# Sliding-window copy: staging in sets of 16 blocks, one per engine, instead of whole batches

## The chip, the cores and the metric

The kernel runs on one core of one Trainium2 chip. The metric is the device time of one execution in microseconds (us); the number that counts is the median of several runs. A core has compute engines (TensorE, VectorE, ScalarE, GpSimd) and a SyncE, and sixteen DMA engines that move all data. SyncE (SP), ScalarE (ACT) and GpSimd (POOL) each start DMAs into a ring of their own; all rings are served by the same sixteen DMA engines. In the profile q1 is SP's ring and q10 is ACT's.

## The reference

x has 32 batches of 4096 rows of 256 float32. A window is 64 rows, the next one starts 32 rows later, so there are 127 windows a batch. The output holds every window in full:

```python
n_windows = (length - window_size) // stride + 1          # 127
for i in range(n_windows):
    start = i * stride
    result[:, i] = x[:, start:start + window_size].copy()
```

Nothing is computed; data is copied. If a batch is cut into 128 blocks of 32 rows (32 KB each), window i consists of blocks i and i+1. Every block but the first and last is written twice: as the second half of one window and as the first half of the next. x is 134 MB, the output 266 MB.

## The kernel before, in words

There are two ways to move a batch, and both run side by side.

*Copied batches* go from HBM to HBM. A window's 64 KB are contiguous in x and in the output, so the copy of a batch is 127 rows of 64 KB whose source rows overlap. It reads 8.32 MB and writes 8.32 MB. `copy` starts three DMAs on SP's ring: 80, 32 and 15 rows, cut into packets of 16, 32 and 16 KB (`COPY_PARTS`, parts of a 64 KB row). A DMA spreads its rows over the DMA engines.

*Staged batches* go through on-chip memory (SBUF). One DMA loads the batch's 128 blocks, one block to a partition (4.19 MB), and two DMAs store the same tile: once as the windows' first halves, once as their second halves, shifted by one block (`half` 0 and -1). A staged batch thus reads 4.19 MB and writes 8.39 MB of HBM, and the DMA engines carry 12.58 MB. All of it is on ACT's ring, in packets of 16 KB. There are five tiles (`BUFS`), each with the semaphores `loaded[i]` and `stored[i]`.

The two stores of a staged batch also write one block beyond it at each end: half -1 of block 0 falls into the last window of the batch before, and half 0 of block 127 into the first window of the batch after it, both with wrong data. So the batches beside a staged one have to be copied after it is stored, or mended afterwards:

- `STAGED` holds the odd batches 1 to 23 (12 of them); the even batches beside them are `near`.
- The four in `EARLY` (18, 20, 22, 24) are copied first of all. Before ACT stores a batch that borders on one, it waits for all early copies. In the end the spoilt half windows (32 KB each) of these are written again, "mended", by seven small DMAs on SP's ring (`g.half`).
- The other near batches are "tied": SP waits for the stores of their staged neighbours (`after_store`) before it copies them. `_order` puts them into SP's list between the free batches, each at a place by when its neighbours should be stored.

ACT's program is a loop over the staged batches: load n+1, wait for load n, store n twice. A load into a tile that was used before waits for its earlier batch's stores. SP's program is the list of copies with the waits of the tied ones, then the mends, then waits for everything and the clearing of the semaphores. Each DMA, when done, adds 16 to its semaphore in all (at most one small completion packet of 4 bytes on each engine).

Of the kernel before, what the change touches and what calls it, by code (L numbers as in the profile page):

```python
# [1 line left out]

# [4 lines left out]


STAGED = tuple(range(1, 24, 2))
BUFS = 5  # L10

EARLY = (18, 20, 22, 24)

BLOCK_PARTS = 2

COPY_PARTS = ((80, 4), (32, 2), (15, 4))


class _Geometry:


    def __init__(self, x, out, W, S):
        self.B, self.L, self.D = x.shape
        self.x, self.out = x, out
        self.n_win = (self.L - W) // S + 1
        self.n_blk = self.L // S
        self.blk = S * self.D
        self.win = W * self.D
        assert W == 2 * S and self.n_blk == self.n_win + 1 == 128

    def src(self, b, block, dims):

        at = (b * self.n_blk + block) * self.blk
        return bass.AP(self.x.tensor, self.x.offset + at, dims)

    def dst(self, b, half, dims):

        at = b * self.n_win * self.win + half * self.blk
        return bass.AP(self.out.tensor, self.out.offset + at, dims)

    def rows(self, b, w0, n):

        s, d = [[self.blk, n], [1, self.win]], [[self.win, n], [1, self.win]]
        return self.dst(b, 2 * w0, d), self.src(b, w0, s)

    def half(self, b, half, block):

        dims = [[self.blk // 16, 16], [1, self.blk // 16]]
        return self.dst(b, half, dims), self.src(b, block, dims)


class _Kernel:
    def __init__(self, nc, g, tiles):
        self.nc, self.g, self.tiles = nc, g, tiles
        self.loaded = [nc.alloc_semaphore(f"loaded{i}") for i in range(len(tiles))]
        self.stored = [nc.alloc_semaphore(f"stored{i}") for i in range(len(tiles))]
        self.copied = nc.alloc_semaphore("copied")
        self.early = nc.alloc_semaphore("early")
        self.count = {}

    def start(self, engine, out, in_, sem, parts=1):
        engine.dma_start(out=out, in_=in_, max_dma_last_dim=65536 // parts).then_inc(sem, 16)
        self.count[id(sem)] = self.count.get(id(sem), 0) + 16

    def all_of(self, engine, sem):
        engine.wait_ge(sem, self.count[id(sem)])

    def slot(self, n):
        return divmod(n, len(self.tiles))

    def after_store(self, engine, n):
        turn, i = self.slot(n)
        engine.wait_ge(self.stored[i], 32 * (turn + 1))

    def load(self, n):

        g, (_, i) = self.g, self.slot(n)
        if n >= len(self.tiles):
            self.after_store(self.nc.scalar, n - len(self.tiles))
        src = g.src(STAGED[n], 0, [[g.blk, g.n_blk], [1, g.blk]])  # L80
        self.start(self.nc.scalar, self.tiles[i][:, :], src, self.loaded[i], 2 * BLOCK_PARTS)

    def store(self, n):

        g, (turn, i) = self.g, self.slot(n)
        self.nc.scalar.wait_ge(self.loaded[i], 16 * (turn + 1))
        for half in (0, -1):
            dst = g.dst(STAGED[n], half, [[g.win, g.n_blk], [1, g.blk]])  # L90
            self.start(self.nc.scalar, dst, self.tiles[i][:, :], self.stored[i], 2 * BLOCK_PARTS)

    def copy(self, b, sem):

        w = 0
        for rows, parts in COPY_PARTS:
            self.start(self.nc.sync, *self.g.rows(b, w, rows), sem, parts)
            w += rows
        assert w == self.g.n_win


def _order(B):


    near = {b for s in STAGED for b in (s - 1, s + 1)}
    order = list(EARLY) + [b for b in range(B) if b not in near and b not in STAGED]
    tied = sorted(near - set(EARLY))
    n = len(order) + len(tied)
    for b in tied:
        behind = max(STAGED.index(s) for s in (b - 1, b + 1) if s in STAGED)  # L110
        order.insert(-(-(2 * behind + 5) * n // (2 * len(STAGED))), b)
    return order


@with_exitstack
def kernel(
    ctx: ExitStack,
    tc: tile.TileContext,
    x: bass.AP,
    window_size: bass.AP,  # L120
    stride: bass.AP,
    out: bass.AP,
):
    nc = tc.nc
    W, S = int(window_size), int(stride)
    g = _Geometry(x, out, W, S)
    assert 0 not in STAGED and g.B - 1 not in STAGED
    pool = ctx.enter_context(tc.tile_pool(name="blocks", bufs=1))
    tiles = [pool.tile([g.n_blk, g.blk], x.dtype, name=f"xb{i}") for i in range(BUFS)]

    with tc.tile_critical():
        k = _Kernel(nc, g, tiles)
        for b in _order(g.B):
            if b not in EARLY:
                for s in (b - 1, b + 1):
                    if s in STAGED:
                        k.after_store(nc.sync, STAGED.index(s))
            k.copy(b, k.early if b in EARLY else k.copied)
        k.load(0)
        waited = False  # L140
        last = len(STAGED) - 1
        for n, s in enumerate(STAGED):
            if n < last:
                k.load(n + 1)
            if not waited and (s - 1 in EARLY or s + 1 in EARLY):
                k.all_of(nc.scalar, k.early)
                waited = True
            k.store(n)


        k.all_of(nc.sync, k.early)
        for n, s in enumerate(STAGED):
            if s - 1 in EARLY or s + 1 in EARLY:
                k.after_store(nc.sync, n)
            if s - 1 in EARLY:
                k.start(nc.sync, *g.half(s - 1, 2 * g.n_win - 1, g.n_blk - 1), k.copied)
            if s + 1 in EARLY:
                k.start(nc.sync, *g.half(s + 1, 0, 0), k.copied)
        for n in range(len(STAGED)):
            k.after_store(nc.sync, n)  # L160
        k.all_of(nc.sync, k.copied)
        for sem in [*k.loaded, *k.stored, k.copied, k.early]:
            nc.sync.sem_clear(sem)


# [1 line left out]
_INS = ['x', 'window_size', 'stride']  # L167
_OUTS = [((32, 127, 64, 256), 'float32')]

_NUMBERS = {'window_size': 64, 'stride': 32}  # L170


# [26 lines left out]
```

## Time and profile before

| What | Value |
|---|---|
| median of 3 runs | 766.97 us (766.28 to 768.57) |
| profiled execution | 768.4 us |
| its span, first to last instruction | 766.6 us |
| bytes moved by the DMA engines | 317.70 MB |
| HBM read / written | 217.02 / 267.35 MB |
| mean rate of the DMA engines | 414 GB/s |
| SP's issues | 20 each of 5120, 2048 and 960 KB, and 7 of 32 KB |
| ACT's issues | 12 loads and 24 stores of 4096 KB |

How to read it: a row of digits gives, for 40 equal slices of the span, the busy share of the sixteen DMA engines in tenths. For each DMA queue the page lists packets (the small completions among them), megabytes and the time that the packets took as a share of sixteen engines' span. The view by windows gives for each stretch the busy time of the compute engines, the granted clock (of no weight here), the DMA engines' busy share, where 1.00 is all sixteen, and GB/s. A wait of the queue's view reads: who waited, on which line, for which DMA; us in total, times, longest.

### The profile page before, as it was taken

The numbers are of one execution on the slowest core, as the hardware profiler recorded it, in microseconds if no ns is written. First come the engines' busy times: TensorE is split into PE (matmuls) and PEld (weight loads), VectorE is DVE, ScalarE is ACT, GpSimd is POOL, SyncE is SP. The second block draws the span as 40 slices with busy tenths as digits, with TensorE's granted clock in tenths as the row PEclk, the third lists the DMA queues.
The fourth block names the chain that finished last, engine by engine and source line by source line (L and its number), as shares of the span: only waits on it lengthen the run. The fifth ranks groups of instructions, "written<-read, shape, count | busy, mean of one in ns | idle before, by whom it ended". The sixth has DMA issues, their size and how long they took to land. (4 is left out here: it accounts for less than half of the span.)

```text
span 766.6 us, 180 instructions
## 1 busy us (share of the span) xinstructions
POOL 0.2 (0%) x4
## 2 busy tenths in 40 slices
POOL 0000000000000000000000000000000000000000
DMA  8999999999999999999999999999999999999996
GB/s 371 425 410 421 405 428 431 408 411 427 423 415 421 431 415 425 432 408 416 427 420 417 431 420 420 423 428 410 414 427 419 422 428 418 417 428 421 420 406 237
DMA packets 19837, 317.70 MB, mean 414 GB/s; under 512 B 1628, under 2 KB 1628, under 8 KB 1740
## 3 DMA queue, kind: packets, MB, share of 16 engines
q1 hardware_dynamic: 10044, 166.70, 51.9%
q10 hardware_dynamic: 9792, 151.00, 47.3%
q14 instruction: 1, 0.01, 0.0%
HBM read 217.02 MB, written 267.35 MB: 632 GB/s over the span
## 5 line engine op out<-in xcount | busy, mean ns | idle before, releaser
L180 POOL MEMSET const-bfloat16-1.0<- 128x1 bf16 x1 | 0.1, 102 | 0.0
L180 POOL MEMSET const-uint8-127<- 128x1 uint8 x1 | 0.1, 102 | 0.0
L180 POOL MEMSET const-float32-0.0<- 128x1 f32 x1 | 0.1, 99 | 0.2 <-issue 0.2
L180 POOL MEMSET const-float32-1.0<- 128x1 f32 x1 | 0.1, 99 | 0.0
## 6 DMA issues: line engine op xcount, KB each, us to landing
out_dram<-in_x_dram SPq DMA_DIRECT2D x20, 5120.0 KB, 114.8
out_dram<-xb ACTq DMA_DIRECT2D x24, 4096.0 KB, 84.6
xb<-in_x_dram ACTq DMA_DIRECT2D x12, 4096.0 KB, 123.2
out_dram<-in_x_dram SPq DMA_DIRECT2D x20, 2048.0 KB, 116.7
out_dram<-in_x_dram SPq DMA_DIRECT2D x20, 960.0 KB, 97.7
out_dram<-in_x_dram SPq DMA_DIRECT2D x7, 32.0 KB, 48.3
```

Source lines behind the costliest of these rows:

```text
L180: nc = _bacc.Bacc("TRN2", target_bir_lowering=False, num_devices=1)
```

## The change

Staging is cut finer. The unit is a set of 16 blocks, every eighth block of a batch (`STEP = 8`, partitions j, j+8, ...), 512 KB, so that one block of 32 KB goes to each DMA engine, as one packet. A batch is eight loads of a set and sixteen stores of one. `_staged` writes out ACT's order: after each load of a set two stores of sets follow, and the loads run ahead of the stores by `AHEAD = 12` sets. There are 13 staged batches (1 to 25), so 19 copied ones, and `EARLY` moves to 20, 22, 24, 26.

A copied batch is now three DMAs on SP's ring of 48, 32 and 32 rows in packets of 16 KB (`GROUPS`, `COPY_PARTS = 4`), and a fourth of its last 15 rows on GpSimd's ring in packets of 32 KB (`copy_others`, `OTHER_PARTS = 2`). GpSimd's DMAs wait for the neighbours as SP's do, and also for a staged batch's stores that paces them (`SLACK = 2`).

The two sets of the last staged batch that spoil its neighbours are stored first of that batch, with a semaphore of their own (`fringe`), and the mends beside that batch wait for that alone. In the end GpSimd, not SP, waits for all semaphores, resets its DMA queue and clears the semaphores in one go.

```diff
-STAGED = tuple(range(1, 24, 2))
+STAGED = tuple(range(1, 26, 2))
 BUFS = 5
-EARLY = (18, 20, 22, 24)
-BLOCK_PARTS = 2
-COPY_PARTS = ((80, 4), (32, 2), (15, 4))
+EARLY = (20, 22, 24, 26)
+STEP = 8
+AHEAD = 12
+GROUPS = (48, 32, 32)
+COPY_PARTS = 4
+OTHER_PARTS = 2
+SLACK = 2
...
-    def start(self, engine, out, in_, sem, parts=1):
+    def start(self, engine, out, in_, sem, parts=2):
         engine.dma_start(out=out, in_=in_, max_dma_last_dim=65536 // parts).then_inc(sem, 16)
...
-        engine.wait_ge(self.stored[i], 32 * (turn + 1))
-
-    def load(self, n):
+        engine.wait_ge(self.stored[i], 2 * 16 * STEP * (turn + 1))
+
+    def load(self, n, j):
         g, (_, i) = self.g, self.slot(n)
-        if n >= len(self.tiles):
+        if j == 0 and n >= len(self.tiles):
             self.after_store(self.nc.scalar, n - len(self.tiles))
-        src = g.src(STAGED[n], 0, [[g.blk, g.n_blk], [1, g.blk]])
-        self.start(self.nc.scalar, self.tiles[i][:, :], src, self.loaded[i], 2 * BLOCK_PARTS)
-
-    def store(self, n):
-        g, (turn, i) = self.g, self.slot(n)
-        self.nc.scalar.wait_ge(self.loaded[i], 16 * (turn + 1))
-        for half in (0, -1):
-            dst = g.dst(STAGED[n], half, [[g.win, g.n_blk], [1, g.blk]])
-            self.start(self.nc.scalar, dst, self.tiles[i][:, :], self.stored[i], 2 * BLOCK_PARTS)
+        src = g.src(STAGED[n], j, [[STEP * g.blk, g.n_blk // STEP], [1, g.blk]])
+        self.start(self.nc.scalar, self.tiles[i][j::STEP, :], src, self.loaded[i])
+
+    def wait_load(self, n):
+        turn, i = self.slot(n)
+        self.nc.scalar.wait_ge(self.loaded[i], 16 * STEP * (turn + 1))
+
+    def store(self, n, j, half, sem=None):
+        g, (_, i) = self.g, self.slot(n)
+        dst = g.dst(STAGED[n], half + 2 * j, [[STEP * g.win, g.n_blk // STEP], [1, g.blk]])
+        self.start(self.nc.scalar, dst, self.tiles[i][j::STEP, :], sem or self.stored[i])
 
     def copy(self, b, sem):
         w = 0
-        for rows, parts in COPY_PARTS:
-            self.start(self.nc.sync, *self.g.rows(b, w, rows), sem, parts)
-            w += rows
+        for n in GROUPS:
+            self.start(self.nc.sync, *self.g.rows(b, w, n), sem, COPY_PARTS)
+            w += n
+
+    def copy_others(self, b, sem):
+        w = sum(GROUPS)
+        self.start(self.nc.gpsimd, *self.g.rows(b, w, self.g.n_win - w), sem, OTHER_PARTS)
...
+def _copies(k):
+    nc, order = k.nc, _order(k.g.B)
+    for c, b in enumerate(order):
+        early = b in EARLY
+        if not early:
+            for n in _beside(b):
+                k.after_store(nc.sync, n)
+        k.copy(b, k.early if early else k.copied)
+        paced = c * len(STAGED) // len(order) - SLACK
+        for n in sorted({n for n in [paced] if n >= 0} | set([] if early else _beside(b))):
+            k.after_store(nc.gpsimd, n)
+        k.copy_others(b, k.early_others if early else k.others)
+
+
+def _staged(k):
+    nc, last = k.nc, len(STAGED) - 1
+    loads = [(n, j) for n in range(len(STAGED)) for j in range(STEP)]
+    stores = [(n, j, half) for n in range(last) for j in range(STEP) for half in (0, -1)]
+    fringe = [(last, STEP - 1, 0), (last, 0, -1)]
+    stores += fringe + [(last, j, half) for j in range(STEP) for half in (0, -1) if (last, j, half) not in fringe]
+    given = 0
+    waited = False
+    for s, (n, j, half) in enumerate(stores):
+        while given < len(loads) and 2 * given <= s + 2 * AHEAD:
+            k.load(*loads[given])
+            given += 1
+        if s % (2 * STEP) == 0:
+            if not waited and any(b in EARLY for b in (STAGED[n] - 1, STAGED[n] + 1)):
+                k.all_of(nc.scalar, k.early)
+                k.all_of(nc.scalar, k.early_others)
+                waited = True
+            k.wait_load(n)
+        k.store(n, j, half, k.fringe if (n, j, half) in fringe else None)
...
+def _end(k):
+    for sem in k.sems:
+        k.all_of(k.nc.gpsimd, sem)
+    k.nc.gpsimd.dma_reset()
+    used = sorted(sem.num for sem in k.sems)
+    assert used == list(range(used[0], used[-1] + 1))
+    k.nc.gpsimd.sem_clear(range(used[0], used[-1] + 1))
```

The function that is left out, `_mends`, holds the mends as they were, with the wait for `fringe` in place of that for the last batch's stores.

## The prediction, made before the changed kernel was run

> **What bounds the kernel now.** I read the page first. No compute engine does any work; the sixteen DMA engines are the kernel.
>
> ```profile
> span 766.6 us, 180 instructions
> DMA  8999999999999999999999999999999999999996
> DMA packets 19837, 317.70 MB, mean 414 GB/s; under 512 B 1628, under 2 KB 1628, under 8 KB 1740
> q1 hardware_dynamic: 10044, 166.70, 51.9%
> q10 hardware_dynamic: 9792, 151.00, 47.3%
> HBM read 217.02 MB, written 267.35 MB: 632 GB/s over the span
> ```
>
> They are busy 99% of the span, so no ring starves: time is bytes divided by rate, plus the two ends. q1 is SP's ring (copies), q10 ACT's (staging). Per byte both are equally dear, yet a staged batch moves 12.58 MB through the engines (one load, two stores) and a copied one 8.32 MB, although the copy costs HBM more (16.65 against 12.58 MB). The question is therefore at what rate the bytes go. The windows tell, once it is known which DMA ACT's ring is in. I counted q10's packets in order (256 data and 16 completions each); the order of issue is load n+1, store n, store n again.
>
> ```profile
> core 0: us, POOL busy (x), PEclk, DMA share, GB/s
> 0.00:6.00 6.00, 0.20 (x4) 1.00 0.68 246
> 6.00:20.00 14.00, 0.00 (x0) 1.00 1.01 432
> 83.00:104.00 21.00, 0.00 (x0) 1.00 1.00 410
> 105.00:125.00 20.00, 0.00 (x0) 1.00 1.01 431
> 146.00:167.00 21.00, 0.00 (x0) 1.00 1.01 404
> 168.00:189.00 21.00, 0.00 (x0) 1.00 1.02 431
> 209.00:231.00 22.00, 0.00 (x0) 1.00 1.00 408
> 232.00:251.00 19.00, 0.00 (x0) 1.00 1.00 429
> 722.00:748.00 26.00, 0.00 (x0) 1.00 0.94 401
> 753.00:764.00 11.00, 0.00 (x0) 1.00 0.59 216
> ```
>
> Windows from 83, 146 and 209 are loads; 105, 168 and 232 are first stores. The share is 1.00 in both, so in load windows the packets themselves take longer. A 16 KB packet takes 611 ns in the clean windows (start to start 607 ns, a 32 KB one 1209 ns); in load phases single packets take 1000 to 1400 ns, the copies' too. The packet records show that the two rings take turns packet by packet, and that a 4-byte completion takes a turn of its own of 6 ns (its record is 9 ns long).
>
> The span adds up. 317.70 MB at 432 GB/s: 735.4 us. Start, 6 us at 246: 2.6 lost. End, 11 us at 216: 5.5, and 2.6 after 764. From about 720 to 753 only fifteen engines work (401 GB/s): 2.4. Together 748.5; the other 18.1 are slow packets in the body: eleven loads, 235 us at about 409, lose 12.5; the first stores, 246 us at 430, lose 1.1; the second stores have the remaining 4.5, mostly in the last 2 us before the ring changes to a load.
>
> Why fifteen engines: q1's 10044 packets are 20 x 444 for copies, 112 for mends, and 1052 completions = 40 x 16 + 7 x 16 + 20 x 15. So each 15-row DMA uses 15 engines, the same ones each time by the idle end.
>
> **The change, part by part.**
>
> *Bytes.* 19 x 8.323 + 13 x 12.583 + 0.23 = 321.95 MB; at 432 GB/s 745.3 us, 9.9 more than now. This is certain and works against the change.
>
> *Completions.* Per engine 312 on ACT, 57 + 7 on SP, 19 on GpSimd: 395 against 103, at 6 ns: 1.8 us more.
>
> *Turns.* 32 KB and a completion on ACT's ring take two turns, in which SP's gets two 16 KB packets: equal bytes, as today. SP has 31 turns a batch, 589 in all; ACT 624. SP's ring runs out first, with some 17 sets (21 us) of stores left to ACT's alone. Today it is the other way round: the end is copies alone, at 216 GB/s while engines finish one by one between 759 and 764. Stores alone ask HBM for half of what copies do; I take 3 us for 5.5 (bounds 2 and 6). The last mends now wait for two sets put first, not for the whole last batch; today's land at 764.8, but other copies run until 763.2, so this gives 1.6 us at most and is in the 3.
>
> *The 15 rows.* If GpSimd's DMAs go round the engines, 2.4 us falls to about 0.5; if they use the same fifteen, 19 x 2 packets x 1.21 us / 16 = 2.9. No POOL DMA is in this trace. With nothing to choose by I take the middle, 1.7, and keep both for the range. [...]
>
> *Issue and waits.* ACT issues 312 DMAs for 36. A store's issue took 378 to 625 ns, so 120 to 195 us of the span, one each 0.6 us at worst where the ring needs one each 2.43 us: hidden. ACT's wait for a set's load has behind it the next sixteen stores, but fifteen sets (36 us of ring) were queued after that load: covered. SP's waits for a stored batch: batch k is stored after 24k+36 sets, at about 58k + 89 us; the copy tied to it comes to SP's ring at 38 us a batch, at least 45 us later in every case (k=9: 612 against 657). SP's existing waits total tens of us in the queue's view and leave the share at 1.00, for the same reason. GpSimd's waits hold only its own 15-row copies, the last of which is free at about 670 us.
>
> ```profile
> SPq L62 <- DMA out_dram<-xb: 61.2, 2, 40.2
> SPq L73 <- DMA out_dram<-xb: 19.2, 3, 9.4
> ```
>
> [...]
>
> *The close.* The queue is reset on GpSimd, which no row shows. Twelve semaphore clears now take 0.7 us. 2.6 becomes 3.5 (bounds 2.2 and 6).
>
> Sum without the body's loss: 745.3 + 1.8 + 2.6 + 3.0 + 1.7 + 3.5 = 757.9 us, against 748.5 today.
>
> *The body's loss, x.* Today loads and stores come in stretches of 20 and 40 us. Half the traffic is copies, so HBM reads and writes are 432 and 216 GB/s in a load stretch, 216 and 432 in a store stretch; mixed as one load to two stores they are 288 and 360. So x is bounded by today's rows: first stores' rate, 0.5% of 720 us, 3.4; all stores, (1.1 + 4.5) / 497, 1.1%, 8; no gain, 18 (what a loss linear in the reads gives too); load stretches' rate, 5.3%, 38. I take 5: 288 is nearer to the clean row, copies suffer too in load stretches (so it is the read load, not the load's own address), and the 4.5 of second stores comes mostly from the change to a load, whose reads then run on for 20 us; one set's reads last 1.2 us.
>
> Span 757.9 + 5 = 762.9. The profiled execution took 768.4, 1.8 over its span and 1.4 over the median of 766.97. So 764.7 beside the profiled 768.4, and 763.3 as median.
>
> **The rivals.**
>
> *No gain from mixing.* x stays at 14 to 20: median 772 to 778. For it: a linear loss; 32-row copies at 32 KB were slow even in store stretches. Against it: first stores lose almost nothing.
>
> *Changes of direction (slower).* Before a load the engines read from HBM for the load while they still write the store. At 82.4 to 83.8 us every packet took 650 to 800 ns: about 0.3 us lost at one change. Now each engine changes 104 times. If all sixteen do it together, 104 x 0.3 = 31 us: 757.9 + 3.4 + 31 is a span of 792.3, a median of 792.7. Spread over the 7.3 us of a load and two stores it costs nothing. It decides the sign where it costs over 766.6 - 757.9 - 3.4 = 5.3 us, 0.05 a change, a sixth of the price. Against lockstep: engines end up to 5 us apart today.
>
> *It doesn't do what it says.* The 15 rows stay on fifteen engines (1.2 us over what I took), and GpSimd's turns raise the copies' part: its two 32 KB packets a batch and engine are 19 x 2 x 1.21 = 46 us of copies, and beside them HBM is asked for more than the mix; at the load stretches' 5.3% that is up to 2.4 us more. Median 764.5 to 767.
>
> **How the numbers follow.** About 0.3% (2.3 us) can be told from no change: under 764.7 is faster, over 769.3 slower. The forecast has 0.55 (0.48 faster, 0.07 same), no gain 0.22, changes of direction 0.13, the last 0.10 (0.02 faster, 0.07 same, 0.01 slower). So faster 0.50, same 0.14, slower 0.36. The forecast's own range is 758 to 767. The whole range must take in no gain: 757 (x near 0 and an even spread of the 15 rows) to 777.
>
> **What would show it.** Right: the windows lie flat at 425 to 431 GB/s with no 20 us dips; q10 has 9984 data-and-completion packets and 163.6 MB; the last 20 us have q10 alone; POOL's ring has 18.2 MB. Wrong: flat windows at or under 420 (changes of direction), a DMA share under 0.98 in the windows of the body (a ring ran dry), or a close over 6 us.

## The result and the profile after

The changed kernel takes 795.76 us (median of 5 runs, 793.61 to 798.17) against 766.97 for the kernel before: a ratio of 1.0377, 95% interval 1.035 to 1.0403. It is slower by 29 us. The forecast was 763.3, with a range up to 777. The profiled execution took 798.17 us, with a span of 796.1.

The page of the changed kernel: the busy digits of the DMA engines, their rate in 40 slices of 19.9 us, the totals and the queues (packets, MB, share of sixteen engines' span). q0 is GpSimd's ring.

```profile
span 796.1 us, 475 instructions
DMA  9999999999999999999999999999999999999994
GB/s 304 344 389 430 424 416 422 429 426 422 434 424 414 424 429 423 430 426 417 431 430 424 431 427 412 428 429 425 431 429 411 427 427 422 424 426 426 351 238 102
DMA packets 20548, 322.00 MB, mean 404 GB/s; under 512 B 6359, under 2 KB 6359, under 8 KB 6471
q10 hardware_dynamic: 9984, 163.60, 51.6%
q1 hardware_dynamic: 9648, 139.69, 41.6%
q0 software_dynamic: 912, 18.68, 5.8%
```

Packets and bytes on every ring are those of the prediction (GpSimd's 18.68 MB where it said 18.2, which had taken 960 KB for 0.96 MB). The engines did not run dry either: the digits are 9 up to the last slice. But the middle is flat at 411 to 434 and the loss stands in the first three slices and the last three. The windows (length, GpSimd's busy time, clock, DMA share, GB/s) show it closer:

```profile
0.00:20.00 20.00, 2.04 (x7) 1.00 0.92 306
20.00:40.00 20.00, 0.00 (x0) 1.00 0.98 339
60.00:80.00 20.00, 0.00 (x0) 1.00 1.01 431
60.00:700.00 640.00, 8.64 (x15) 1.00 1.01 425
742.00:760.00 18.00, 0.00 (x0) 1.00 1.03 298
762.00:776.00 14.00, 0.00 (x0) 1.00 1.01 246
```

The share is 1.01 at 246 GB/s: the engines are occupied all the time, with packets that take up to twice as long. The kernel before ran at 421 from 60 to 700 us. So the body's rate did rise, by 1%; the two ends lose far more.

From 762 to 776 us the rings show who is there:

```profile
q10 hardware_dynamic: 202, 3.31, 98.1%
q1 hardware_dynamic: 128, 0.13, 2.7%
```

ACT's ring is all but alone, with stores of sets. A 32 KB store takes 2168 ns there on average in the packet records (median 2458), where the median is 1213 in the body. In the first 45 us, where ACT's ring holds loads of sets only, a load takes 1570 to 2490 ns (mean of a set), although SP's and GpSimd's packets go between.

The span in one sum, from the packet records. "Slow packets" is the time of packets over 611 ns (16 KB), 1213 (32 KB) and 84 (2 KB), divided by sixteen engines; "rest" is engines that end unevenly, and before the change the engine without 15-row copies.

| us | before | changed |
|---|---|---|
| first packet starts | 2.0 | 2.3 |
| bytes at 432 GB/s | 735.4 | 745.2 |
| completions (6 ns a turn) | 0.6 | 2.4 |
| slow packets, 0 to 80 us | 2.5 | 9.8 |
| slow packets, 80 to 720 us | 15.6 | 10.0 |
| slow packets, from 720 us | 1.2 | 17.5 |
| rest | 6.5 | 6.6 |
| last packet ends | 763.8 | 793.9 |
| to the span's end | 2.8 | 2.2 |

Of 30 us, 9.9 are bytes, 1.8 completions, 7.3 slow packets at the start and 16.3 at the end; the body gives 5.6 back.

### The profile page after: what moved, and what is told of

It reads as the page before. It is cut to its first block, busy times and chain, and to the rows that moved or that the text cites. A ratio compares the mean times of both kernels' runs of the same rounds, so it can differ in the third digit from the quotient of the medians.

```text
span 796.1 us, 475 instructions
## 1 busy us (share of the span) xinstructions
POOL 11.3 (1%) x23
## 3 DMA queue, kind: packets, MB, share of 16 engines
q0 software_dynamic: 912, 18.68, 5.8%
## 4 chain that ended last, share of the span: by engine, by line
another core or an unknown queue 44%; ACTq 30%; DMA 14%; issue 1%; SPq 0%
ACTq L75 30%; DMA xb<-in_x_dram 14%; ACTq L98 0%; ACTq L251 0%; SPq L215 0%
## 5 line engine op out<-in xcount | busy, mean ns | idle before, releaser
L75 POOL DMA_DIRECT2D out_dram<-in_x_dram x19 | 11.1, 583 | 696.9 <-DMA out_dram<-xb 695.8
```

## The experiments

Three causes could make packets slow at both ends. *Completions*: a ring that is alone must wait after each packet for its completion. *Distance*: sixteen engines work on blocks 256 or 512 KB apart and meet in HBM. *Packet size*: 32 KB packets are slow alone.

**Patterns alone, and beside copies.** Two kernels, each run once, held nothing but stretches of 8.39 MB on ACT's ring, the second with 112 rows of a batch's copy beside each. A stretch is written as

```python
for j in range(step):                                  # step 0: eight sets of 16 adjoining blocks
    dma(tile[j::step, :], x_block(b, j::step), parts)  # loads; step 1 is a whole batch in one DMA
```

> Twelve stretches on ACT's ring alone, one after the other, each 8.39 MB in 32 KB blocks; it moves only these blocks and no copies. Loads: sets of every eighth block in 32 KB packets; whole batches in 32 KB packets; whole batches in 16 KB packets; sets of 16 adjoining blocks; sets of every eighth block in 16 KB packets. Stores: the same first four, then sets of every fourth block (two packets before a completion), sets of every eighth in 16 KB packets, sets of every second block (four packets before a completion). At 432 GB/s a stretch lasts 19.4 us. Completion theory: a ring that is alone waits after each packet that is followed by a completion, about 1.3 us as in the changed kernel's last stretch (2.54 us for a 1.21 us packet). Then sets take 16 x 2.5 = 40 us whatever the distance of the blocks and the packet size, every fourth block about 30, every second about 25, whole batches 20 to 22. Distance theory: sixteen engines on blocks 256 or 512 KB apart at the same time meet in HBM. Then whole batches, which have the same distance between engines, are as slow as the sets (40 us), and adjoining blocks take 20. Packet theory: 32 KB packets are slow alone: everything in 32 KB takes 40, everything in 16 KB 20.

The windows of the kernel with ACT's ring alone (GB/s last; the edges of a stretch are cut off), in the order of the text above:

```profile
3.00:43.00 40.00, 0.00 (x0) 1.00 0.95 198
45.00:65.00 20.00, 0.00 (x0) 1.00 0.93 400
67.00:87.00 20.00, 0.00 (x0) 1.00 0.96 410
89.00:160.00 71.00, 0.00 (x0) 1.00 0.97 113
163.00:203.00 40.00, 0.00 (x0) 1.00 1.01 210
206.00:246.00 40.00, 0.00 (x0) 1.00 0.94 197
248.00:267.00 19.00, 0.00 (x0) 1.00 0.97 414
269.00:288.00 19.00, 0.00 (x0) 1.00 1.01 428
290.00:351.00 61.00, 0.00 (x0) 1.00 0.88 131
353.00:372.00 19.00, 0.00 (x0) 1.00 1.03 442
375.00:415.00 40.00, 0.00 (x0) 1.00 0.97 203
417.00:436.00 19.00, 0.00 (x0) 1.00 0.97 414
```

All three causes fall. Over its whole stretch a set of every eighth block runs at 207 GB/s, loads and stores alike, in 32 and in 16 KB packets: not the packet size. Adjoining blocks, which were to be the cure, are slowest, at 117 and 136: not the distance. Whole batches, at 403 to 423, say less of it than was meant: the records name no partition and no address, so which blocks the engines hold at one moment is not known. Sets of adjoining blocks have as many completions as sets of every eighth and run at 117 and 136 for 207, and 32 blocks in one DMA (every fourth block), with one completion for two packets, run at 426 instead of the 280 that a wait of 1.3 us a completion would give: not completions. What orders the rows seems to be where the blocks lie on chip. 207 and 117 are about a half and a quarter of 432, as if half of the sixteen engines, or a quarter, moved data at a time (an estimate from these rates).

> The same patterns on ACT's ring (five of loads, six of stores, without the last one), each beside the copy of 112 rows in 16 KB packets on SP's ring; nothing else is moved. At 432 GB/s 8.39 + 7.34 MB take 36.4 us. It asks why the changed kernel's first 40 us, all loads of sets beside copies, ran at 290 to 350 GB/s with loads at 1.8 to 2.0 us a packet. Completion theory: the other ring's packets fill the wait, so all patterns take 37 to 39 us, and the slow start needs another cause (GpSimd's ring, or loads alone). Distance theory: sets of every eighth block and whole batches are slow alike (45 us or more for loads), adjoining blocks are not. Packet theory: 32 KB patterns slow, 16 KB ones not.

Windows of that kernel: sets of every eighth block loaded, whole batches in 32 KB, whole batches in 16 KB, adjoining blocks loaded, adjoining blocks stored.

```profile
3.00:55.00 52.00, 0.00 (x0) 1.00 0.95 294
58.00:96.00 38.00, 0.00 (x0) 1.00 0.96 402
98.00:135.00 37.00, 0.00 (x0) 1.00 0.98 420
137.00:222.00 85.00, 0.00 (x0) 1.00 0.95 181
404.00:462.00 58.00, 0.00 (x0) 1.00 0.86 262
```

The first is like the changed kernel's start (306 and 339), without GpSimd: copies between do not heal it. Stores of sets lose less beside copies, 371 GB/s over their stretch.

**Two parts of the changed kernel undone.**

> The changed kernel with the last 15 rows of a copied batch on SP's ring, behind its other copies, in 32 KB packets; GpSimd starts no DMA. SP's ring then has 19 x 34 = 646 turns an engine against ACT's 624, so that ACT's ring is never left alone for long. Theory that the end (stores alone at 235 GB/s) costs about 20 us and the start about 10: the end goes, 2.4 us come back as fifteen engines carry the 15 rows, and copies alone end it as in the kernel before (about 3 us): 775 to 782. Rival, that the sets themselves cost the time wherever they are, and the end is only where it shows: 790 or more.

```diff
-        self.start(self.nc.gpsimd, *self.g.rows(b, w, self.g.n_win - w), sem, OTHER_PARTS)
+        self.start(self.nc.sync, *self.g.rows(b, w, self.g.n_win - w), sem, OTHER_PARTS)
```

(GpSimd's waits and the reset of its queue go with it.) Ratio 1.0284 (1.023 to 1.0338), some 789 us, from three executions of 786.19 to 794.32 us: neither expectation. The profile is of a fourth, of 803.77 us. In it the slow packets from 720 us are 4.5 us for 17.5, as ACT's ring is no longer left alone, and the slow start stays (12.7 us in the first 80). But a single engine works from 783 to 798 us; whether the shorter executions end so too, and so where their time went, is open.

> The changed kernel with the first two staged batches loaded by one DMA each, in 16 KB packets, and all else in sets. It asks for the start alone: the changed kernel loses about 12 us in its first 60. If the slow start comes of loads in sets (completions or packets of 32 KB): 785 to 788. If it comes of sixteen engines that start together on blocks 256 KB apart, or of GpSimd's four early copies: 794 to 797.

```diff
     def load(self, n, j):
+        if n < WHOLE:                                      # WHOLE = 2
+            if j == 0:
+                src = self.g.src(STAGED[n], 0, [[self.g.blk, self.g.n_blk], [1, self.g.blk]])
+                self.start(self.nc.scalar, self.tiles[n][:, :], src, self.loaded[n], 4)
+            return
```

The wait for these loads is changed to match. 792.11 us, ratio 1.0317 (1.0292 to 1.0342). In its windows the start is healed to 351 and 413 GB/s, with GpSimd's early copies in place, and the end is not:

```profile
0.00:20.00 20.00, 2.04 (x7) 1.00 0.91 351
20.00:40.00 20.00, 0.00 (x0) 1.00 1.00 413
742.00:760.00 18.00, 0.00 (x0) 1.00 1.02 268
```

Slow packets in the first 80 us fall from 9.8 to 4.5. The time falls by 3.7, less than the 8 to 11 expected: I had taken the whole of the start for it.

**The place on chip.** The new theory, "port theory" in the expectations that follow, is that the rate goes by where on chip the blocks lie that the sixteen engines hold at the same moment; a "port" there is a name for places that hold each other up. How the place acts no run shows.

> Twelve stretches on ACT's ring alone, all in sets of 16 blocks of 32 KB; it moves only these blocks and no copies. First loads: every eighth block in the order 0 to 7; every eighth in the order 0, 4, 1, 5, 2, 6, 3, 7; every fourth (16 blocks within one half of the partitions); every second; every seventh (14 sets); again the second. Then stores, two halves each, in the same order of patterns. [...] Rival, that the engines stay in step whatever the order: the new order as slow as the old, 207.

It ran once. Loads of every eighth block in order, in the new order, every fourth, every second, every seventh; then the stores of the same:

```profile
3.00:43.00 40.00, 0.00 (x0) 1.00 0.95 197
45.00:83.00 38.00, 0.00 (x0) 1.00 1.00 221
86.00:126.00 40.00, 0.00 (x0) 1.00 0.95 198
128.00:168.00 40.00, 0.00 (x0) 1.00 0.97 202
171.00:199.00 28.00, 0.00 (x0) 1.00 0.91 245
241.00:281.00 40.00, 0.00 (x0) 1.00 0.94 197
283.00:317.00 34.00, 0.00 (x0) 1.00 0.93 233
320.00:359.00 39.00, 0.00 (x0) 1.00 0.94 202
361.00:401.00 40.00, 0.00 (x0) 1.00 0.98 205
403.00:426.00 23.00, 0.00 (x0) 1.00 0.90 319
```

Over their whole stretches, sets of 16 blocks run alike at 206 to 209 GB/s, loads and stores, whether they take every eighth, every fourth or every second block; every seventh is faster, 258 for loads and 312 for stores, and adjoining blocks, in the first of the two kernels above, had 117 and 136. So if the partitions set the rate, it is not by their distance alone: 2, 4 and 8 are alike, 7 is not. The new order brought little, 218 GB/s for loads and 239 for stores, where the rival has 207: the sixteen packets of each of its sixteen sets of loads start within 1.0 us of one another, so the engines stay in step.

A rival has to be met here: a block's number sets its place in HBM as well as its partition, so the rows could be HBM's. But a store's blocks lie twice as far apart in HBM as a load's. At 64 KB apart, loads (every second block) run at 206 and stores (adjoining blocks) at 136, while loads and stores of the same partitions run at 206 and 207 (every second, and every eighth) and at 208 and 209 (every fourth); the pairs 117 and 136 (adjoining) and 258 and 312 (every seventh) are wider, but in the same order. So HBM distance does not order the rows, and partitions do. Two things are open. How a DMA of more than 16 blocks is dealt to the engines no record shows, and so not why every fourth block ran at 426 GB/s in DMAs of 32 and at 209 in sets of 16. And what it is in the partitions that sets the rate, no run shows.

Next comes the changed kernel with one thing changed, the order of a batch's sets, for loads and stores alike: its sets in a row then lie three or four partitions apart, not one.

> [...] Port theory: the slow start (10 us) and the slow end (17 us) go, the body's 10 us stay or shrink: 766 to 773. Rival, that engines meet in HBM or wait for completions whatever the set's place on chip: no change, 793 to 797.

```diff
-    loads = [(n, j) for n in range(len(STAGED)) for j in range(STEP)]
-    stores = [(n, j, half) for n in range(last) for j in range(STEP) for half in (0, -1)]
+    loads = [(n, j) for n in range(len(STAGED)) for j in TURN]      # TURN = (0, 4, 1, 5, 2, 6, 3, 7)
+    stores = [(n, j, half) for n in range(last) for j in TURN for half in (0, -1)]
```

779.9 us, ratio 1.016 (1.0136 to 1.0184), between the two expectations: 16 us of the 29 come back by the order of the sets alone, with each set's DMA as it was (the last batch's are reordered in the same way, but for the two that go first).

```profile
0.00:20.00 20.00, 2.04 (x7) 1.00 0.92 306
20.00:40.00 20.00, 0.00 (x0) 1.00 0.98 338
742.00:760.00 18.00, 0.00 (x0) 1.00 1.03 390
```

The end runs at 390 for 298, and its slow packets are 2.4 us for 17.5. By then the engines have drifted apart (in the changed kernel they end one by one: the packets in flight fall from 16 to 2 between 777 and 792 us), so that they can be in different sets at one moment. The start is untouched in this profile, at odds with the expectation and in line with the stretch alone. It need not be: the kernel with the new order and 12 batches, further down, begins with the same loads and ran at 406 from 20 to 40 us, with 5.3 us of slow packets for 9.9.

> The changed kernel with sets of 32 blocks, every fourth block, two for each engine (the loads run ahead by 6 sets, the same bytes). [...] Port theory: as with the new order, 764 to 773; half as many completions, 0.9 us less. ACT's ring then has three turns for 64 KB in place of four, so it gets more of the engines and SP's ring is the longer one: copies alone at the end, 3 to 6 us. Rival (completions): half of the loss stays, 780 to 785.

The edit is `STEP = 4` and `AHEAD = 6`. 791.02 us, ratio 1.0309 (1.0293 to 1.0324): as slow as the rival, or slower, and for another reason. ACT's three turns for 64 KB gave it so much of the engines that it ended at 699 us, and copies alone ran for 89 us more, where I had said 3 to 6 us in all:

```profile
60.00:690.00 630.00, 9.22 (x16) 1.00 1.01 424
702.00:780.00 78.00, 0.00 (x0) 1.00 0.99 323
```

The start was healed (slow packets 4.1 for 9.8).

> As the kernel with the new order, with 12 staged batches in place of 13 (and 18, 20, 22, 24 copied early, as in the kernel before). 4.3 MB less at 432 GB/s: 9.9 us less; SP's ring becomes the longer one (620 turns against 576), copies alone at the end for some 20 us, where HBM is the limit: 3 to 6 us more. Port theory: 5 us under the new order with 13 batches, 760 to 768, and under the kernel before if the body's loss stays at 10 us. Rival, that in the mixed body 13 batches are needed to spare HBM: no faster than with 13.

778.91 us, ratio 1.0128 (1.0097 to 1.016). Not the 760 to 768 expected, and no faster than with 13, as the rival has it, though its reason is not thereby shown: the bytes are 9.9 us fewer, and hardly 1 us of it shows. SP's ring ran 27 us longer than ACT's (777.4 against 749.9), copies alone; that HBM limits these is not shown. Against the new order with 13 batches the slow packets are 4.6 us fewer at the start, but 3.7 more in the body and 4 more from 720 us, and the engines end less evenly.

**What the parts are worth, and a better version.**

> The kernel before with 13 staged batches (and 20, 22, 24, 26 copied early) and nothing else: the price of the added bytes alone. 4.3 MB at 432 GB/s are 9.9 us. ACT's ring then has 663 turns an engine against SP's 589, so that stores alone end it; whole-batch stores ran at 416 to 423 GB/s alone, so that costs no more than today's end. Bytes theory: 774 to 779. Rival, that 13 batches pay because HBM is spared: 767 or less.

The edit is `STAGED` to 26 and `EARLY = (20, 22, 24, 26)` in the kernel before. 777.03 us against 767.68, ratio 1.0117 (1.0104 to 1.013): 9.4 us, the bytes.

> The changed kernel with both mends of its ends: sets in the order 0, 4, 1, 5, 2, 6, 3, 7, and the first two staged batches loaded whole. If start and end are separate losses at the ports, the gains add (16 us and 4 us): 773 to 777. What is left over the kernel before is then the bytes (9.9) and the completions (1.8), less the body's gain (about 5). Rival: the ring's place in phase carries over from the start to the end, and the gains don't add: 778 to 790.

777.46 us, ratio 1.0126 (1.0111 to 1.0141). Slow packets: 3.7, 10.6 and 4.4 for start, body and end. With both ends mended, the changed kernel is as fast as the kernel before with 13 batches, whose three are 2.1, 14.6 and 0.1: what the body gains goes to the ends and to 1.7 us of completions.

> As the last one, with 12 staged batches and SP's copies as 96 rows in 16 KB and 16 rows in 32 KB packets, so that SP's ring has 560 turns and ACT's 578; the last 15 rows are on GpSimd's ring as in the changed kernel. From the sum: 735.7 for bytes, 2 for completions, 2.3 start, 12 slow packets, 4 uneven end, 2.5 close: span 759, median 760 (757 to 765), faster than the kernel before by 0.5 to 1.2%. Rival: the mixed body's gain of 5 to 8 us is eaten by the completions and by uneven ends: 765 to 772.

```diff
-GROUPS = (48, 32, 32)
+GROUPS = ((96, 4), (16, 2))            # rows, parts
```

> As the last one, without GpSimd: the 15 rows are SP's last, in 32 KB packets, after 80 rows in 16 KB and 32 in 32 KB; SP's ring has 580 turns on fifteen engines and ACT's 578. Against the one with GpSimd's ring: 2.4 to 2.9 us more for the fifteen engines, 1 to 2 less for the stretches in which three rings take turns: 759 to 766. Rival: GpSimd's ring brings nothing, equal within 1 us or faster without it.

Both staged 12 batches, with the new order and the whole first loads; the second has `GROUPS = ((80, 4), (32, 2))`. With the 15 rows on GpSimd's ring: 766.48 us, ratio 0.9979 (0.9962 to 0.9996). On SP's: 765.49, ratio 0.9975 (0.9954 to 0.9996). Both are 0.2% under the kernel before, with intervals that just leave out no difference. The first lies in its rival's range of 765 to 772, the second at the far end of its own: with 12 batches and rings that end together the mixed body (slow packets 13.4 and 10.2 us for 15.6) is worth little more than its completions and its start cost. GpSimd's ring brings nothing that can be measured.

## Why the prediction was wrong, by its own steps

*Bytes: right.* 9.9 us predicted; 9.4 measured with nothing else changed.

*The end: the step that failed.* The prediction saw that 17 sets of stores would be left to ACT's ring alone, asked only what HBM would say to that, and took 3 us with bounds of 2 and 6. From 742 to 794 us the engines moved 218 GB/s: 26 us lost at the prediction's 432, of which slow packets are 17.5 (from 720 us on) and engines that end one by one most of the rest. The count of sets was right: SP's last copies landed between 744 and 752 us, and ACT then had about as many sets left; but they went at 238 GB/s (752 to 776 us), and the last landed 42 us after the copies, where 21 were reckoned. No row of the trace before had a 16-partition DMA, or ACT's ring alone but for the first 4 us; the bounds came from another pattern, copies, and should have been marked as such. The sets' place on chip was never weighed, although the diff shows it (partitions j, j+8, ...): such stores ran at 207 GB/s alone.

*The start: the same omission.* 2.6 us were carried over unchanged; slow packets in the first 80 us rose from 2.5 to 9.8, as 13 loads of sets stand at the head of ACT's ring, and such loads run at 206 GB/s alone. The new order shows that the end goes by the order of the sets (390 GB/s for 298), the whole loads that the start comes of loads in sets (413 for 339); together they give 18.3 of the 18.7 us by which the changed kernel is over the old one with 13 batches.

*The body's loss x: it fell, but by less than half of what was forecast.* 5 us were taken, between 3.4 and 8, for 18.1. Slow packets from 80 to 720 us fell from 15.6 to 10.0, and the rate rose from 421 to 425, not to the first stores' 430. No run parts the mixing from the larger packets that came with it. That the leftover comes of the sets' place on chip is not shown either: ACT's traffic in the body is about half of 432, little over what sets of every eighth block reached alone (207), but the new order left it at 11.2.

*Issue, waits, close: right.* GpSimd waited 696 us for stores and held up nobody; the share stays at 1.01 in the body; from the last packet to the end it is 2.2 us, not 3.5.

*The 15 rows.* Of the two kernels with 12 mixed batches, the one with the 15 rows on SP's ring has the plateau of fifteen engines (DMA share 0.93, 392 GB/s from 720 to 738 us), the one with GpSimd's ring has not (1.01, 431). So GpSimd's DMAs do not leave out the same engine each time, but the pair shows no gain in time, and the term of 1.7 us was not measured.

*The rivals.* The slower one, changes of direction, named 792.7 us and the time is 795.76, but that is chance: it put the loss into the body, as 104 changes, and the body got faster. The rival of no gain priced only the body too. None of them contained the ends. The signs named for being wrong did not appear either: the body is over 420, its share is not under 0.98, and the close is under 6 us.

## What to carry to other kernels

Sixteen busy engines are not yet the full rate (DMA share 0.95 at 198 GB/s, loads of every eighth block alone): write down, for each DMA that touches on-chip memory, which partitions its blocks lie in, and time that pattern alone. Of the sets of 16 blocks, every seventh ran at 258 and 312 GB/s for the 206 and 207 of every second and every eighth; no whole kernel was run with it. Another order of the sets is the weaker remedy: it gave 390 for 298 GB/s with the engines apart, 218 for 206 with the engines in step. A pattern may be harmless in the mix and cost double where its ring is alone or the engines are in step (425 GB/s in the changed kernel's body, 246 from 762 to 776 us), so price the first and the last 50 us of a kernel with their own pattern and not with the body's rate. And when rings take turns packet by packet, count turns: the ring with more of them is left alone at the end, at its own rate (ACT with 624 turns against 589, SP with 589 against 468 in the kernel with sets of 32).

## What the runs showed of the hardware

In sets of every eighth block alone, loads and stores, a packet that takes 1.21 us in the body takes 2.5, while the record still counts the engine as busy (share 0.95), so the DMA share says nothing of it. Engines that start in step stayed in step for 16 sets (218 GB/s in the new order alone), but are spread at the end of the kernel (the changed kernel's engines ended between 777 and 794 us). Copies from HBM to HBM alone moved 323 GB/s through the engines, 646 GB/s at HBM, reads and writes together; the clean windows of half copies and half staging, 432 GB/s, come to 648 by the same reckoning (an estimate). That HBM is what holds the copies is not shown; the likeness of the two sums may be why no mix ran faster. A completion after every 32 KB packet cost little more than its turn of 6 ns while packets were not slow (431 GB/s from 60 to 80 us of the changed kernel). On GpSimd's ring each DMA left 18 of the 4-byte packets (342 for 19).
